# Memory cross-attention planned on all engines at once, and head 0 of its queries by plain products

## The chip, the cores and the metric

The kernel runs on one core of one Trainium2 chip. The metric is the device time of one execution in microseconds (us). Three runs of the kernel before gave 1443.65 to 1445.43 us, with a median of 1444.97 us.

The engines are named as in the profile: PE (TensorE, matmuls; PEld is its weight load), DVE (VectorE), ACT (ScalarE), POOL (GpSimd) and SP (SyncE, whose queue issues most of the DMAs; POOL issues those that add to what is in the tile already).

## What is computed

One sequence of 512 tokens with 1024 channels goes through two layers. Each has a mixer (attention of two kinds in layer 0, an mLSTM in layer 1), a cross-attention to a memory of 256 tokens, and a gated feed-forward part with a short convolution. The change is in the cross-attention, which has 4 heads of 256 channels:

```
def memory_cross_attention(xn, memn, wq, wkv, wo):
    q = split_heads(xn @ wq, XATTN_HEADS)
    k, v = jnp.split(memn @ wkv, 2, axis=-1)
    k = split_heads(k, XATTN_HEADS)
    v = split_heads(v, XATTN_HEADS)
    logits = jnp.einsum('bhqd,bhmd->bhqm', q, k, preferred_element_type=jnp.float32) * (XATTN_HEAD_DIM ** -0.5)
    p = jax.nn.softmax(logits, axis=-1)
    out = jnp.einsum('bhqm,bhmd->bhqd', p.astype(v.dtype), v)
    return merge_heads(out) @ wo
...
x = x + memory_cross_attention(rms_norm(x, xattn_norm[layer]), rms_norm(mem, mem_norm[layer]), ...)
```

## The kernel before

**Products.** Activations lie with channels on the 128 partitions: `x` is eight tiles `x0` to `x7` of 128x512. Every operand of a product is split into a high part of type fp32r and the rest, so that a product is three matmuls (`mm3`, lines 374 to 380: high by high, low activation by high weight, high activation by low weight). A block of 128 output channels needs a weight tile of 128x1024, which goes through three steps: a DMA into a `raw` tile, a cast on ACT into `wh`, a subtraction on DVE into `wl`. There are three buffers each of `raw`, `wh` and `wl`. PE writes to four banks `acc0` to `acc3`, and to two each of `s` and `w`.

**The stage.** In each layer the cross-attention begins where the mixer's output product ends. That product's last block gives `x7`: DVE adds it (`xadd`), ACT writes `xh7` and a square, DVE writes `xl7` and sums the squares (`xprep`). The stage has these parts:

- Values: two blocks of 512 channels, each from four weight tiles of `in_xv`, with `mem` as the other operand (`p_proj_tok`, lines 440 to 442, 512 columns a matmul), kept as `xvh` and `xvl`.
- Keys: eight blocks of 128 channels from `in_xk`. Four of them are computed within the mixer already (`p_fill`) and wait in two `acc` banks; DVE scales them (tile `u`), ACT and DVE split them into `kt`. The other four are computed within the stage.
- Queries: eight blocks of 128 channels from `in_xq`, two for each head. A pair of blocks is computed with seven products of half size instead of eight (`p_seven`, 256 columns a matmul). It needs sums of the pair's weight halves: the tile `sa`, loaded by SP and added to by a DMA of POOL, the tile `sb0` or `x0`, formed by DVE and added to by another DMA of POOL, and a plain half loaded into `x5`. It also needs sums of the activations' halves (`form`: tiles `q`, then `pth`, `ptl` and `mixed`). As the tiles of `x` serve as room for these weights, `x` is written to DRAM first (`xs`) and read back later.
- For each head and each 128 queries: scores (`s`), their maximum (`sm`), the exponential (`xe`), its division by the sum, a transposition (line 1393), the weighting of the values (`w`).
- Output: eight blocks from `in_xo`, added to `x`, whose parts the feed-forward part uses.

**What sets the order.** `Plan` (line 111) holds the stage's steps with a priority and a duration on PE, and a chain of what follows on ACT and DVE. It keeps a clock for PE, takes the ready step of the best priority, and calls its function, which issues the instructions of all engines at once. Priorities are written out: values `VP` = 5, the four pairs 10, 20, 30 and 40, weights of a pair `PREP` = 19 earlier, keys `KP` = 57, scores 55 to 85, output 100. The order that results is not fixed within an engine: the builder moves instructions of different steps against each other. The feed-forward part is ordered by another planner, `Sched` (line 208): each instruction or group is a task of its own engine with a duration, a due time, the tasks it needs and the buffers it takes and frees, and the order that it finds is fixed on ACT, DVE and POOL (`nc.planned(True)`).

Of the kernel before, what the change touches and what calls it, by code (L numbers as in the profile page):

```python
# [16 lines left out]
P = 128  # L17
SEQ = 512
# [66 lines left out]
KP = 57  # L85
PREP = 19
VP = 5
FORM_AT, FORM_STEP = 2.0, 5.0


class Busy:

    def __init__(self, free):
        self.free, self.spans = free, []

    def place(self, at, d):
        at = max(at, self.free)
        k = 0  # L100
        for k, (a, b) in enumerate(self.spans):
            if at + d <= a:
                break
            at = max(at, b)
        else:
            k = len(self.spans)
        self.spans.insert(k, (at, at + d))
        return at + d


class Plan:
# [3 lines left out]
    def __init__(self, prev=None, hold=(), gaps=False, **res):  # L115
        self.gaps = gaps
# [13 lines left out]
    def run(self):  # L130
        todo = sorted(self.items, key=lambda i: (i.prio, i.n))
        eng, t = self.eng, self.t
        busy = {e: Busy(min(eng[e], t + 0.5)) for e in eng}

        def place(e, at, d):
            if self.gaps:
                return busy[e].place(at, d)
            eng[e] = max(eng[e], at) + d
            return eng[e]

        while todo:
# [27 lines left out]
            for e, d in pick.pre:  # L169
                place(e, t - 4.0, d)  # L170
# [3 lines left out]
            for e, d in pick.chain:  # L174
                if e == "-":
                    u += d
                    continue
                u = place(e, u, d) + 0.06
                clear = clear or u
            for e, d in pick.load:  # L180
                place(e, t, d)
# [25 lines left out]

class Sched:
# [3 lines left out]
    def __init__(self, **res):  # L212
        self.tasks = []
# [9 lines left out]
    def slot(self, r):  # L223

        s = self.slots[r]
        if r == "acc":
            return min(range(len(s)), key=lambda i: s[i])
        return self.turn[r] % len(s)

    def run(self):  # L230
        order = sorted(self.tasks, key=lambda t: (t.prio, t.n))
# [7 lines left out]
        now = {e: -AHEAD.get(e, 0.0) for e in todo}  # L239
        inf = float("inf")  # L240
        idle = 0.0
        while any(todo.values()):
            best = None
            for e, ts in todo.items():
                soon, pick = inf, None
                for t in ts[:120]:
# [9 lines left out]
                    for r, _ in t.take:  # L256
# [3 lines left out]
                        at = max(at, self.slots[r][self.slot(r)])  # L260
# [66 lines left out]
class Builder:  # L327
# [830 lines left out]
    def form(self, layer, k, to, scratch):  # L1158

        nc, tt = self.nc, self.nc.vector.tensor_tensor  # L1160
        hi, lo, raw = (v[:].rearrange("p a b -> p (a b)") for v in to)
        for j in range(2):
            nc.scalar.activation(scratch[:, j, :], self.x[k + 4 * j][:], AF.Identity, scale=self.col("xat", layer * 8 + k + 4 * j))
        T1, T3, T2, T4 = (raw[:, 256 * i : 256 * i + 256] for i in range(4))
        x0, x1 = ([scratch[:, j, 256 * i : 256 * i + 256] for i in range(2)] for j in range(2))
        tt(out=T1, in0=x0[0], in1=x0[1], op=ALU.subtract)
        tt(out=T3, in0=x1[1], in1=x0[1], op=ALU.subtract)
        nc.vector.scalar_tensor_tensor(out=T2, in0=T1, scalar=-1.0, in1=x1[1], op0=ALU.mult, op1=ALU.subtract)
        nc.vector.scalar_tensor_tensor(out=T4, in0=T2, scalar=-1.0, in1=x1[0], op0=ALU.mult, op1=ALU.subtract)
        self.split(hi, lo, raw)  # L1170

    def p_seven(self, pl, pair, mp, X, T, formed, kdeps, done, prio, before, turn):
# [1022 lines left out]
```

## Time and profile before

| what | us |
|---|---|
| median of three runs | 1444.97 |
| profiled execution | 1446.33 |
| its span, first to last instruction | 1444.4 |
| PE busy within the span | 1411.4 |
| DVE, ACT, POOL busy | 1178.2, 865.8, 152.8 |
| cross-attention of layer 0 on PE | from 252.44 to 409.19 |
| cross-attention of layer 1 on PE | from 951.45 to 1107.23 |

The profile is that of one execution. A row of the timeline gives the start of an instruction, its duration, its engine and line, the tile written and those read, and in brackets the idle time before it with what ended it. Matmuls overlap, so that their durations add up to more than they take: a matmul's price is the distance between starts. A row of the windows gives the busy time of each engine in a stretch, and the clock that was granted to PE (1.00 is full). Times count from the span's start.

### The profile page before, as it was taken

The numbers are of one execution on the slowest core, as the hardware profiler recorded it, in microseconds if no ns is written. First come the engines' busy times: TensorE is split into PE (matmuls) and PEld (weight loads), VectorE is DVE, ScalarE is ACT, GpSimd is POOL, SyncE is SP. The second block draws the span as 40 slices with busy tenths as digits, with TensorE's granted clock in tenths as the row PEclk, the third lists the DMA queues.
The fourth block names the chain that finished last, engine by engine and source line by source line (L and its number), as shares of the span: only waits on it lengthen the run. The fifth ranks groups of instructions, "written<-read, shape, count | busy, mean of one in ns | idle before, by whom it ended". The sixth has DMA issues, their size and how long they took to land.

```text
span 1444.4 us, 23191 instructions
## 1 busy us (share of the span) xinstructions
PE 1411.4 (98%) x8732; PEld 1271.1 (88%) x8732; DVE 1178.2 (82%) x2018; ACT 865.8 (60%) x1456; POOL 152.8 (11%) x205
## 2 busy tenths in 40 slices
PE   9999999799999999999999999988999999999998
PEld 8888869699889999999888888877988899999997
DVE  7887776767789999999768867676767999999984
ACT  6797554555566665666456654464556666656654
POOL 0003220300001011110001121020000011110100
PEclk9999999899999999999999999999999999999999
DMA  5225325754148776774233332566504777676622
GB/s 203 87 67 162 95 86 188 214 139 146 60 143 216 187 186 173 190 181 120 74 113 110 117 110 66 168 198 173 174 5 136 206 198 191 176 187 170 158 74 80
DMA packets 78304, 206.85 MB, mean 143 GB/s; under 512 B 8449, under 2 KB 8449, under 8 KB 78193
## 3 DMA queue, kind: packets, MB, share of 16 engines
q1 hardware_dynamic: 62432, 163.97, 34.4%
q0 software_dynamic: 14752, 40.30, 16.0%
q8 instruction: 68, 1.11, 0.3%
q10 hardware_dynamic: 1008, 1.12, 0.2%
q14 instruction: 44, 0.35, 0.1%
HBM read 199.01 MB, written 6.34 MB: 142 GB/s over the span
## 4 chain that ended last, share of the span: by engine, by line
PE 83%; DVE 6%; ACT 3%; issue 3%; DMA 3%; POOL 1%; POOLq 0%; DVEq 0%; ACTq 0%; SPq 0%
PE acc L378 16%; PE acc L379 16%; PE acc L380 16%; PE w L379 5%; PE w L378 5%; PE w L380 5%; PE s L378 3%; PE s L380 3%; PE s L379 3%; PE acc L440 2%; PE acc L442 2%; PE acc L441 2%; DVE wl L300 1%; ACT wh L300 1%; PE w L1971 1%
## 5 line engine op out<-in xcount | busy, mean ns | idle before, releaser
L300 ACT CAST wh<-raw 128x1024 fp32r<-128x1024 f32 (+2 forms) x221 | 226.4, 1026 | 186.6 <-PE acc L379 94.7
L300 DVE TENSOR_TENSOR wl<-raw,wh 128x1024 fp32r<-128x1024 f32 (+2 forms) x221 | 264.4, 1198 | 40.9 <-ACT wh L300 40.5
L378 PE MATMUL acc<-xh,wh 128*128 128x512 f32 (+1 forms) x736 | 244.6, 332 | 0.0
L379 PE MATMUL acc<-xl,wh 128*128 128x512 f32 (+1 forms) x736 | 243.0, 330 | 0.0
L380 PE MATMUL acc<-xh,wl 128*128 128x512 f32 (+1 forms) x736 | 243.0, 330 | 0.0
L380 PEld LDWEIGHTS acc<-xh,wl 128*128 128x128 f32 x736 | 140.7, 191 | 10.2
L378 PEld LDWEIGHTS acc<-xh,wh 128*128 128x128 f32 x736 | 140.8, 191 | 10.0 <-DVE x L300 0.3
L379 PEld LDWEIGHTS acc<-xl,wh 128*128 128x128 f32 x736 | 140.8, 191 | 9.4
L300 DVE SCALAR_TENSOR_TENSOR c<-hs,vec,c 128x512 f32<-128x512 f32 x176 | 131.8, 749 | 3.8 <-ACT c L300 0.8
L378 PE MATMUL w<-ah,wh 128*128 128x512 f32 x304 | 115.7, 381 | 0.2 <-ACT c L300 0.2
L379 PE MATMUL w<-al,wh 128*128 128x512 f32 x304 | 115.2, 379 | 0.0
L380 PE MATMUL w<-ah,wl 128*128 128x512 f32 x304 | 115.2, 379 | 0.0
L300 ACT ACTIVATE c<-hs,vec 128x512 f32<-128x512 f32 x88 | 70.8, 812 | 12.2 <-DVE hs L300 8.0
L300 ACT CAST ah<-c 128x512 fp32r<-128x512 f32 x44 | 27.3, 620 | 84.0 <-DVE c L300 83.9
L300 DVE TENSOR_TENSOR x<-acc,x 128x512 f32<-128x512 f32 (+1 forms) x43 | 27.9, 653 | 52.9 <-PE acc L380 52.9
L378 PEld LDWEIGHTS w<-ah,wh 128*128 128x128 f32 x304 | 57.6, 190 | 7.9 <-DVE x L300 0.9
L380 PEld LDWEIGHTS w<-ah,wl 128*128 128x128 f32 x304 | 57.5, 189 | 8.1
L300 POOL TENSOR_TENSOR y<-z,power 128x4 f32<-128x4 f32 (+1 forms) x17 | 31.5, 1855 | 305.4 <-DVE z L300 305.3
L379 PEld LDWEIGHTS w<-al,wh 128*128 128x128 f32 x304 | 57.6, 190 | 6.5
L378 PE MATMUL acc<-mem,wh 128*128 128x256 f32 (+1 forms) x192 | 60.4, 315 | 2.8 <-ACT wh L300 2.7
L300 DVE TENSOR_TENSOR wl<-sa,wh 128x1024 fp32r<-128x1024 f32 x44 | 53.8, 1223 | 10.2 <-ACT wh L300 10.1
L300 POOL DMA_DIRECT2D sa<-in_up_dram x36 | 31.4, 873 | 279.6 <-DMA sa<-in_up_dram 121.9
(429 smaller groups left out, 4177.2 us busy)
## 6 DMA issues: line engine op xcount, KB each, us to landing
raw<-in_up_dram SPq DMA_DIRECT2D x52, 512.0 KB, 4.1
sa<-in_up_dram SPq DMA_DIRECT2D x36, 512.0 KB, 3.6
sa<-in_up_dram POOLq DMA_DIRECT2D x36, 512.0 KB, 6.5
raw<-in_down_dram SPq DMA_DIRECT2D x32, 512.0 KB, 4.0
ra<-in_up_dram SPq DMA_DIRECT2D x36, 256.0 KB, 4.3
sb<-in_up_dram POOLq DMA_DIRECT2D x36, 256.0 KB, 5.0
raw<-in_wo_dram SPq DMA_DIRECT2D x16, 512.0 KB, 4.2
raw<-in_xk_dram SPq DMA_DIRECT2D x16, 512.0 KB, 3.6
```

Of the source, the lines that this page charges most:

```text
L300: i = issue(*a, **k)
L378: mm(out, wh, xh, start=first, stop=False, skip_group_check=parts)
L379: mm(out, wh, xl, start=False, stop=False, skip_group_check=parts)
L380: mm(out, wl, xh, start=False, stop=last, skip_group_check=parts)
L440: mm(ps, xh[k][:, ts], wh, start=(k == 0), stop=False)
L441: mm(ps, xh[k][:, ts], wl, start=False, stop=False)
L442: mm(ps, xl[k][:, ts], wh, start=False, stop=(k == 7))
L1971: nc.tensor.matmul(ps[:, lo:], vv[s][:, c], a[:], start=(s == 0), stop=(s == 3))
```

## The change

The planner `Sched` gets three things. A task may take two buffers of one kind at once. Due times of ACT, DVE, POOL and SP tasks are no longer those written by hand but are computed (`dues`): a task's latest useful time is the earliest latest time of those that need it, or its buffer, less its duration; PE tasks keep theirs. And an engine may wait (`WAIT`, 0.4 us for DVE, 0.3 for ACT) for a task that is due earlier, instead of taking the first that can start.

The cross-attention is written anew as tasks of this planner (`xattn_steps`), with its own order of the PE work: 16 half-weight steps of the values (the first `ONE` = 4 come before the activations' sums in the list, the other `TWO` = 12 after), then head 0, then the pairs of heads 1, 2 and 3 by seven products with key blocks or the scores of head 0 between them, then transpositions and scores in turn with the weighting, then the output. Head 0 is now computed by plain products (`plain`): two weight tiles of `in_xq`, each with 24 matmuls of 512 columns, and no sums. The order is fixed on ACT, DVE and POOL for the whole stage. The mixers and the feed-forward parts stay as they were. `Plan` loses the search for gaps between planned spans.

In each layer PE has 36 instructions less in this stage, and DVE 8 less. The core of the diff:

```diff
+WAIT = {"DVE": 0.4, "ACT": 0.3}
+ONE, TWO, FORM, THEN = 4, 12, 10.0, (2, 1, 1)
...
+    def dues(self):
+        after = {t.n: [(c, 0.0) for c in ()] for t in self.tasks}
+        for t in self.tasks:
+            for d in t.deps:
+                after[d.n].append((t, 0.0 if d.eng == t.eng else d.lat))
...
+        def last(t):
+            if t.n not in late:
+                late[t.n] = t.prio
+                ends = [last(c) - lat for c, lat in after[t.n]]
+                if ends and t.eng != "PE":
+                    late[t.n] = min(ends) - t.dur
+            return late[t.n]
...
-                    if at < soon - 1e-6:
-                        soon, pick = at, t
-                if pick is not None and (best is None or soon < best[0]):
-                    best = (soon, e, pick)
+                    able.append((at, t))
+                if able:
+                    near = min(at for at, _ in able) + self.wait.get(e, 0.0) + 1e-6
+                    soon, pick = next((at, t) for at, t in able if at <= near)
...
+        sc = Sched(
+            WAIT, raw=3, h=3, sa=2, sb=2, ra=1, s2=1, a22=1, s4=1, qc=1, v=1, u2=1, u3=1, kx=1, q=6, kt=3, e=7, pt=2, acc=4, s=2, w=2
         )
+        sc.slots.update(h=[-10.4, -5.2, 0.0])
...
+            return add("SP", 0.0017 * cols, fn, (), at, [(tag, st)], (), 4.0)
...
+        sc.ahead = {**AHEAD, "ACT": 10.4, "DVE": 10.4}
+        for at in (-10.4, -5.2, 0.0):
+            add("DVE", 0.65, None, (), -40.0, after=at + 0.2)
+            add("ACT", 1.2, None, (), -40.0, after=at + 1.0)
+            add("DVE", 1.3, None, (), -40.0, after=at + 1.8)
+        XLAST = 3.0
...
+        def keys(m, get, deps, free=()):
...
+                st["x"] = self.til(mp, "kx", (P, MEM), bufs=1)
+                tt_(out=folded(st["x"][:]), in0=restored(get()), in1=folded(self.memrb[:]), op=ALU.mult)
...
+        def plain(p):
+            sts, qs, los = [], ({}, {}), []
+            for j in range(2):
+                st, lo = weight(t["xq"][layer, 2 * p + j], clock[0])
+                last = None
+                for c in range(4):
...
+                        for k in (2 * c, 2 * c + 1):
+                            w = slice(k * P, (k + 1) * P)
+                            self.mm3(st["ps"][:], st["wh"][:, w], st["wl"][:, w], self.xh[k], self.xl[k], k == 0, k == 7)
+                    last = pe(1.297, fn, [lo, last], [("acc", st)] if c == 0 else (), [("h", st)] if c == 3 else ())
...
+        some(ONE)
+        for k in range(4):
+            f, a, st = form(k, FORM + 4.0 * k)
...
+        some(TWO)
+        for _ in plain(0):
+            pass
+        got.append(seven(1, lambda i: some(THEN[i])))
+        got.append(seven(2, lambda i: scores(0, i)))
+        scores(0, 3)
+        got.append(seven(3, lambda i: some((2, 1, 1)[i])))
...
+        for m in range(8):
+            for _ in out_block(m):
+                pass
+        nc.planned(True)
+        sc.run()
+        nc.planned(False)
```

In the new kernel the DVE multiplication that scales a key block writes a tile `kx` with one buffer, where the kernel before had four buffers `u`.

**How the order moves.** Outside the two stages the order of the engines stays the same, but for a few instructions where the stage meets the feed-forward part. The number behind a name tells which of many tiles of that name it is; line 300 in the kernel before and line 306 in the new one are the helper that records each operation of DVE, ACT and POOL.

On DVE, where the stage begins in layer 0, the kernel before has the following rows. `wl_2808` is the low part of the first value weight, `x_144` is `x7` with the addition of the mixer's output, the four `u` are the key blocks that wait in `acc`, and `z` is a small step of the normalization.

```order
L300 SCALAR_TENSOR_TENSOR xl_555_2696<-x_142,vec,xh_554_2695 128x512
L300 TENSOR_TENSOR x_143<-acc_553_2688,x_143 128x512
L300 TENSOR_TENSOR wl_2808<-raw_2806,wh_2807 128x1024
L300 SCALAR_TENSOR_TENSOR xl_562_2736<-x_143,vec,xh_561_2735 128x512
L300 TENSOR_TENSOR sq_2551<-sq_2551,sqt_2739 128x512
L300 TENSOR_TENSOR x_144<-acc_560_2728,x_144 128x512
L300 TENSOR_TENSOR u_2786<-acc_512_2421,memrb_1933 128x256
...
L300 SCALAR_TENSOR_TENSOR xl_565_2763<-x_144,vec,xh_564_2762 128x512
L300 TENSOR_TENSOR sq_2551<-sq_2551,sqt_2766 128x512
L300 TENSOR_TENSOR kt_2785<-u_2786,kt_2785 128x256
...
L300 TENSOR_TENSOR wl_2853<-raw_2851,wh_2852 128x1024
```

In the new kernel the same place reads as follows; the first value weight is `wl_2809`, and `kx` is the tile that takes the place of `u`.

```order
L306 SCALAR_TENSOR_TENSOR xl_562_2736<-x_143,vec,xh_561_2735 128x512
L306 TENSOR_TENSOR sq_2551<-sq_2551,sqt_2739 128x512
L306 TENSOR_TENSOR x_144<-acc_560_2728,x_144 128x512
L306 TENSOR_TENSOR kx_2804<-acc_512_2421,memrb_1933 128x256
L306 TENSOR_TENSOR wl_2809<-raw_2797,wh_2808 128x1024
L306 SCALAR_TENSOR_TENSOR xl_565_2763<-x_144,vec,xh_564_2762 128x512
L306 TENSOR_TENSOR sq_2551<-sq_2551,sqt_2766 128x512
L306 TENSOR_TENSOR kt_2803<-kx_2804,kt_2803 128x256
L306 TENSOR_TENSOR kx_2816<-acc_512_2421,memrb_1933 128x256
L306 TENSOR_TENSOR wl_2821<-raw_2799,wh_2820 128x1024
```

The first value weight's subtraction moved from a place ahead of the addition of `x7` to one behind it and behind the first key block's multiplication. The second value weight's moved from a place behind all four key blocks' splitting to one behind the first block's.

On SP's queue at the same place the kernel before has these rows; `sa` are the loads of the pairs' sums, `xs` is the copy of `x7` to DRAM, and `x_625` is a plain half.

```order
L363 DMA raw_2869<-in_xv_dram 128x1024
L1209 DMA sa_2776<-in_xq_dram 128x2x512
L1209 DMA sa_2803<-in_xq_dram 128x2x512
L1289 DMA xs_633_3005<-x_144 128x512
L1230 DMA x_625_2985<-in_xq_dram 128x512
L363 DMA raw_2903<-in_xv_dram 128x1024
L363 DMA raw_2932<-in_xv_dram 128x1024
L363 DMA raw_3007<-in_xv_dram 128x1024
L363 DMA raw_3025<-in_xv_dram 128x1024
L363 DMA raw_3043<-in_xv_dram 128x1024
```

In the new kernel the same place of SP's queue has these.

```order
L1193 DMA sa_2806<-in_xq_dram 128x2x512
L1193 DMA sa_2812<-in_xq_dram 128x2x512
L1193 DMA raw_2818<-in_xv_dram 128x1024
L1304 DMA xs_665_3096<-x_144 128x512
L1193 DMA raw_2826<-in_xv_dram 128x1024
L1193 DMA raw_2855<-in_xv_dram 128x1024
L1193 DMA raw_2884<-in_xv_dram 128x1024
L1193 DMA x_644_3003<-in_xq_dram 128x512
L1193 DMA raw_2913<-in_xv_dram 128x1024
L1193 DMA raw_2954<-in_xq_dram 128x1024
```

Three value weights moved ahead of the plain half, and behind the last of them the weight of head 0 (`raw_2954` from `in_xq`) follows at once.

On POOL the kernel before has these rows in the stage of layer 0: the sums that its DMAs add (`sa`, `sb`) and the small root of the normalization (`y`).

```order
L300 DMA sa_2776<-in_xq_dram 128x1024
L300 DMA sa_2803<-in_xq_dram 128x1024
L300 TENSOR_TENSOR y_2832<-z_2831,power 128x4
L300 DMA sb_608_2915<-in_xq_dram 128x512
L300 DMA sa_3090<-in_xq_dram 128x1024
```

In the new kernel they are these.

```order
L306 DMA sa_2806<-in_xq_dram 128x1024
L306 DMA sa_2812<-in_xq_dram 128x1024
L306 DMA x_658_3069<-in_xq_dram 128x512
L306 TENSOR_TENSOR y_3144<-z_3143,power 128x4
L306 DMA sa_3140<-in_xq_dram 128x1024
```

The first addition to a half (`x_658`) moved ahead of the root, and the root stands behind three DMAs in place of two.

More of the change, by code (lines that the diff above doesn't have):

```diff
@@ L84, with __init__ @@
 HOLD = 4.0
[L85 to L108, printed above, removed]
 class Plan:
-    def __init__(self, prev=None, hold=(), gaps=False, **res):
-        self.gaps = gaps
+    def __init__(self, prev=None, hold=(), **res):
         self.items = []
@@ L238, in run @@
                 want[r].append(t)
-        now = {e: -AHEAD.get(e, 0.0) for e in todo}
+        now = {e: -self.ahead.get(e, 0.0) for e in todo}
         inf = float("inf")
```

658 lines of the change are left out of this document (420 added, 238 removed).

## The prediction

> **What bounds the kernel now.** First the page's head, for the execution's length and each engine's load.
>
> ```profile
> span 1444.4 us, 23191 instructions
> PE 1411.4 (98%) x8732; PEld 1271.1 (88%) x8732; DVE 1178.2 (82%) x2018; ACT 865.8 (60%) x1456; POOL 152.8 (11%) x205
> ```
>
> PE is busy for 98% of the span, so the change can only gain in two ways: less work for PE, or PE's work done without gaps and without lost clock. The whole span's share doesn't tell where the cross-attention stands, so I went next to PE's timeline, for the first matmul of the stage (line 440) and the first of the feed-forward part (line 378 with `xh`), in both layers.
>
> ```profile
> 252.44 0.38 PE L440 MATMUL acc<-wh,mem 128*128 128x512 f32 x1
> ...
> 409.19 0.38 PE L378 MATMUL acc<-xh,wh 128*128 128x512 f32 x1
> ...
> 951.45 0.38 PE L440 MATMUL acc<-wh,mem 128*128 128x512 f32 x1
> ...
> 1107.23 0.38 PE L378 MATMUL acc<-xh,wh 128*128 128x512 f32 x1
> ```
>
> The stage takes 409.19 − 252.44 = 156.75 us in layer 0 and 155.78 in layer 1. What it would take without any loss needs the price of a step. Four rows of the same timeline, each pair inside a run of matmuls of one size, give it as a distance of starts.
>
> ```profile
> 239.71 0.38 PE L379 MATMUL acc<-ml,wh 128*128 128x512 f32 x1
> 251.79 0.38 PE L378 MATMUL acc<-qa,wh 128*128 128x512 f32 x1
> ...
> 321.89 0.28 PE L379 MATMUL acc<-ptl,x 128*128 128x256 f32 x1
> 323.90 0.28 PE L379 MATMUL acc<-mixed,x 128*128 128x256 f32 x1
> ```
>
> Fifty-six steps of 512 columns lie between the first two (12.08 / 56 = 0.2157 us), eighteen of 256 columns between the others (2.01 / 18 = 0.1117 us). By the code the stage has 336 steps of 512 columns (values 96, output 192, weighting 48): 72.5 us. It has 528 of 256 columns (four pairs of 84, keys 96, scores 96): 59.0 us. Transpositions and small sums add an estimated 4.4, from the size of their outputs. Together 135.9, so 20.9 us are lost in layer 0 and 19.9 in layer 1. Where they are lost the windows tell (columns: stretch, length, busy PE, PEld, DVE, ACT, POOL, PE's clock, DMA share, GB/s).
>
> ```profile
> core 0: us, PE busy (x) PEld busy (x) DVE busy (x) ACT busy (x) POOL busy (x), PEclk, DMA share, GB/s
> 252.40:292.00 39.60, 32.05 (x140) 26.89 (x140) 29.61 (x50) 23.38 (x33) 11.26 (x5) 0.83 0.72 201
> 292.00:344.00 52.00, 50.21 (x431) 48.85 (x430) 37.31 (x65) 30.52 (x56) 3.42 (x4) 1.00 0.60 175
> 344.00:409.20 65.20, 64.16 (x339) 55.63 (x338) 44.64 (x99) 32.39 (x69) 0.14 (x2) 1.00 0.23 74
> 409.20:442.00 32.80, 32.80 (x157) 28.86 (x156) 31.79 (x52) 23.93 (x32) 2.96 (x3) 1.00 0.54 161
> 259.70:264.70 5.00, 5.00 (x12) 3.96 (x13) 4.83 (x9) 2.68 (x4) 5.00 (x1) 0.50 1.04 268
> 279.20:285.20 6.00, 6.00 (x26) 5.82 (x27) 4.39 (x6) 3.13 (x4) 0.84 (x1) 0.50 0.69 156
> ...
> 951.40:992.00 40.60, 32.74 (x148) 26.79 (x148) 31.15 (x51) 24.32 (x35) 11.42 (x5) 0.87 0.75 216
> ```
>
> The first 40 us hold the loss: PE idle for 39.60 − 32.05 = 7.55 us (7.86 in layer 1), and at half clock for 5.0 + 6.0 us, which costs another 5.5. The other two windows are idle for 1.79 and 1.04 us; the remaining 20.9 − 7.55 − 5.5 − 2.83 ≈ 5.0 must lie in gaps that the modelled ends of matmuls cover. The fourth window is the feed-forward part, ordered by the planner that now gets this stage: no idle time at all. What ends the waits is in PE's waits of the first window and in its timeline, with layer 1's longest.
>
> ```profile
> PE acc L440 <- ACT wh L300: 4.1, 1, 4.1
> PE acc L441 <- DVE wl L300: 3.1, 2, 2.5
> ...
> 256.15 1.05 PE L537 MATMUL s<-ones,sq 128*128 128x2 f32 x8 [0.33 <-DVE sq L300]
> 259.70 0.79 PE L441 MATMUL acc<-wl,mem 128*128 128x512 f32 x1 [2.50 <-DVE wl L300]
> 279.16 1.22 PE L440 MATMUL acc<-wh,mem 128*128 128x512 f32 x2 [4.14 <-ACT wh L300]
> 304.33 0.38 PE L378 MATMUL acc<-mem,wh 128*128 128x256 f32 x1 [1.66 <-ACT wh L300]
> ...
> 987.79 0.48 PE L441 MATMUL acc<-wl,mem 128*128 128x512 f32 x1 [3.28 <-DVE wl L300]
> ```
>
> PE waits for value weights: their splitting on DVE is late, or their raw tile is. So the stage's beginning is bound by the preparation of weights, the rest by PE.
>
> **The change, part by part.** *Plain head 0.* Seven products are 84 × 0.1117 = 9.38 us, the plain pair 48 × 0.2157 = 10.35: PE gets 0.97 us a layer more, and the new floor is 136.8 us. The sums of head 0, one POOL DMA of 512 KB and one of 256 KB are gone; DVE and ACT, 29.61 and 23.38 of 39.60 us busy there, get lighter just where they are late. I cost that at nothing beside the 0.97.
>
> *Start of the stage.* These rows of DVE and ACT give the durations.
>
> ```profile
> 248.34 1.23 DVE L300 TENSOR_TENSOR wl<-raw,wh 128x1024 fp32r<-128x1024 f32 x1 [0.18 <-ACT wh L300]
> 252.64 0.69 DVE L300 TENSOR_TENSOR x<-acc,x 128x512 f32<-128x512 f32 x1 [1.82 <-PE acc L380]
> 253.25 1.41 DVE L300 TENSOR_TENSOR u<-acc,memrb 128x256 f32<-128x256 f32 x4
> ...
> 252.43 1.05 ACT L300 CAST wh<-raw 128x1024 fp32r<-128x1024 f32 x1 [2.99 <-PE acc L379]
> ```
>
> Before, the first value weight's subtraction ran at 248.34, while the mixer's product still occupied PE. Now it stands behind the addition of `x7`, which cannot start before 252.64, and behind one key block's multiplication. It ends at 252.64 + 0.61 (distance to the next start) + 0.35 (a quarter of 1.41) + 1.23 = 254.8. PE wants it after two steps, at 252.9: a wait of about 2.0 us, which is new and comes once a layer. Queued behind it on DVE are `xl7` and the sum of squares, which the normalization needs; nobody on PE needs those before the first pair or plain head, some 40 us on.
>
> *The other value weights.* Before, the next one was subtracted only behind all four key blocks and part of the sums (row at 259.70: a wait of 2.50). Now only the first block stands ahead of it, so this wait goes, and the half clock behind it. Next late is the ring of three raw tiles. Each weight feeds 12 × 0.2157 = 2.59 us of matmuls, so a round of three is 7.8 us. A raw tile's round is its landing, a cast of 1.05, a subtraction of 1.23 and about 0.2 between: the landing plus 2.5. The landings, by DMA issues of the raw tiles from 225 to 330 us, were these (all raw tiles, then value weights alone).
>
> ```profile
> DMA to landing us min/median/max: 3.1/3.8/6.2
> ...
> raw<-in_xv_dram SPq DMA_DIRECT2D x8, 512.0 KB, 4.9
> ```
>
> With 4.9 the ring's round is 7.4 us, below 7.8, and holds; with 6.2 it is 8.7. DVE's own work from the addition of `x7` to the last value weight is eight subtractions at 1.23 and about 10 us of splitting and sums in some 21 us; it nearly fills the time. I book one further slip of 1.2 us, an estimate from that tightness: 2.0 + 1.2 = 3.2 us lost here, between 2 (the ring never late) and 10 (late each round).
>
> *Middle and end.* Before, 1.79 + 1.04 us of idle time and 5.0 hidden were lost. DVE is busy for 37.31 of 52.00 and 44.64 of 65.20 us there; a planned order should find PE's work in time, as in the fourth window, but the end (weighting, then output) runs through DVE and ACT a head at a time, and its short gaps are of the kind that stay. I keep the 2.8 and a third of the 5.0: 4.5, with 2 and 8 as ends.
>
> *POOL.* Its additions to the tiles of the pairs now stand around the root `y` in another order (first `x`, then `y`, then the third `sa`). The rows that price it, and the same root in the feed-forward part:
>
> ```profile
> 257.59 7.83 POOL L300 TENSOR_TENSOR y<-z,power 128x4 f32<-128x4 f32 x1
> ...
> 415.97 1.21 POOL L300 TENSOR_TENSOR y<-z,power 128x4 f32<-128x4 f32 x1 [36.62 <-DVE z L300]
> ```
>
> A DMA queued behind it waits for up to 7.83 us. The first pair's products come only after 41 us of values and 10 us of plain products, so I take nothing; the other end is the last rival.
>
> *Sum.* Lost after: 3.2 + 4.5 = 7.7 us a layer. Layer 0 gains 20.9 − 7.7 − 0.97 = 12.2, layer 1, which loses the same way, 19.9 − 7.7 − 0.97 = 11.2; together 23.4. The profiled execution, 1446.33 us (span 1444.4 and 1.9 around it), would be 1422.9. It lies 1.36 above the median of the runs, so the median becomes **1421.6 us**. By the ends of the terms, 4 to 18 us lost a layer, it is 1414 to 1442; both at their far end together is unlikely, and the forecast's own range is 1414 to 1430.
>
> **Rivals.** *The new first wait halves the clock.* For it: the wait of 2.50 us did (0.50 until 264.70), and 2.0 is not far off. Against: the wait of 1.66 at 304.33 lies in a window whose clock is 1.00. Just ahead of the 2.50 stood a microsecond of tiny sums (row at 256.15), which the new wait doesn't have. Price as there, 5.0 us at half clock, so 2.5 a layer: 1426.6. [...]
>
> *Transfers in each other's way.* SP now issues value weights, `sa`, the plain half and the weights of head 0 closely, where the DMA share was 1.04 already in one stretch. With landings of 6.2 the ring loses 0.9 us on each of its remaining two rounds, and the waits may reach 4 with one stretch at half clock (3.0 us): about 9.4 us lost at the start in place of 3.2, so 6.2 a layer more: 1434.
>
> *All is better placed than I think.* Start 2, rest 2: 3.7 us a layer less, 1414, and somewhat lower if the ring's wait vanishes with it.
>
> *The freed time is not PE's to use.* The end runs through DVE and ACT, which gain little; if gaps there take what the start frees, the kernel stays at 1445. Against: 44.64 of 65.20 us on DVE.
>
> *Slower: the sums of the pairs come late.* Place: POOL's queue, where the third `sa` stands behind `y`, and the `x` that SP loads wait for the copy of `x7`. If the root is asked for late, or its 7.83 us repeat at each turn, the pairs' products wait. It decides from the point where a sum lands over 2.5 us after PE has reached its product, for then the clock halves too. Three pairs at the 4.14 us of the longest wait with its 3.0 us of half clock are 21 us; with 4 us at the start and 4.5 at the end a layer loses 29.5 + 0.97, against 20.9 and 19.9: about 10 us a layer slower, 1465.
>
> **How the numbers follow.** Forecast 0.52; better than it 0.12; half clock 0.12; transfers 0.10; no use 0.06; slower 0.08. The median of three runs here spreads by 1.8 us, so 0.2% (2.9 us) is about what a measurement can tell from no change. Faster by more than that takes the first four, 0.86, less some for their upper ends that reach 1442 and beyond: 0.83. Within it 0.06; slower 0.11, the last rival and 0.03 of those ends. The range takes the forecast, most of the better case, half clock and transfers: 1411 to 1438.
>
> **What would show it.** Right: the stages at about 144.5 us each; a wait of about 2 us for the first `wl` right at the stage's start and none over 2.5 behind it; clock 1.00 from the second value weight on; PE idle below 5 us in the first 40; the matmuls of head 0 0.2157 us apart. Wrong: a stage above 150 us; waits of line 380's products for `sa` or `x` that POOL adds to; DVE over 90% busy at the end with PE waiting for it; any change outside the two stages by more than 2 us.

## The result, and the profile after

The changed kernel took 1424.22 us (median of four runs, 1422.05 to 1424.72) against 1444.31 (four runs of the kernel before); the ratio is 0.9858, with a 95% interval of 0.984 to 0.9875. That is 20.1 us less. The prediction was 1421.6 us, 23.4 less than the median it started from.

The page of the changed kernel begins so.

```profile
span 1422.3 us, 22959 instructions
...
PE 1399.5 (98%) x8660; PEld 1263.0 (89%) x8660; DVE 1169.5 (82%) x2006; ACT 859.9 (60%) x1444; POOL 138.4 (10%) x201
```

PE's timeline gives the stage as before; line 1375 is now the first matmul of the values, and the second and fifth row are the first of head 0's plain products.

```profile
254.45 0.38 PE L1375 MATMUL acc<-wh,mem 128*128 128x512 f32 x1
...
281.96 0.38 PE L384 MATMUL acc<-xh,wh 128*128 128x512 f32 x1
...
398.35 0.38 PE L384 MATMUL acc<-xh,wh 128*128 128x512 f32 x1
...
940.61 0.38 PE L1375 MATMUL acc<-wh,mem 128*128 128x512 f32 x1
...
968.12 0.38 PE L384 MATMUL acc<-xh,wh 128*128 128x512 f32 x1
...
1084.51 0.38 PE L384 MATMUL acc<-xh,wh 128*128 128x512 f32 x1
```

The stage takes 143.90 us in both layers, where it took 156.75 and 155.78: 12.85 and 11.88 less, 24.7 together. Between the stages the two kernels take the same 542.26 us. The spans differ by 22.1, since in this execution the first stage begins 2.01 us later than in that of before (254.45 against 252.44) and the part behind the second takes 0.6 more. The experiments below begin the first stage between 252.03 and 253.12, but for e12, whose stage begins with a gap. The 2.01 us arise well ahead of the stage, 0.8 of them before 13 us, where both kernels run the same code; why, no run shows. So medians that differ by some 2 us need not differ in the stage, and below the length of the stage stands beside the median where it matters.

The windows of the stage in layer 0, and the start of the one in layer 1, show where.

```profile
core 0: us, PE busy (x) PEld busy (x) DVE busy (x) ACT busy (x) POOL busy (x), PEclk, DMA share, GB/s
254.40:294.90 40.50, 36.21 (x177) 30.38 (x177) 35.66 (x55) 28.07 (x39) 4.38 (x4) 1.00 0.74 217
294.90:344.00 49.10, 49.06 (x429) 48.53 (x428) 36.94 (x84) 30.73 (x65) 3.37 (x4) 1.00 0.56 165
344.00:398.30 54.30, 54.05 (x268) 47.29 (x267) 36.78 (x72) 25.68 (x48) 0.17 (x2) 1.00 0.24 78
...
940.60:981.00 40.40, 36.38 (x176) 30.22 (x175) 35.69 (x55) 28.18 (x39) 4.38 (x4) 1.00 0.74 210
```

PE's clock is 1.00 in all of them, where the first window had 0.83. PE's idle time in the first window falls from 7.55 to 4.29 us, in the second from 1.79 to 0.04, in the third from 1.04 to 0.25. In the first window DVE is now busy for 88% of the time in place of 75%: the same engine has less empty time in the part where PE waits for it.

What is left at the start stands in PE's waits of the first window (us in total, times, longest).

```profile
PE acc L1376 <- DVE wl L306: 2.7, 4, 1.0
PE acc L1375 <- ACT wh L306: 1.0, 1, 1.0
PE acc L1375 <- DVE x L306: 0.6, 1, 0.6
```

The first two of them in PE's timeline:

```profile
255.40 0.48 PE L1375 MATMUL acc<-wh,mem 128*128 128x512 f32 x1 [0.57 <-DVE x L306]
256.86 0.48 PE L1376 MATMUL acc<-wl,mem 128*128 128x512 f32 x1 [0.98 <-DVE wl L306]
```

And DVE's timeline at the same place:

```profile
254.65 0.69 DVE L306 TENSOR_TENSOR x<-acc,x 128x512 f32<-128x512 f32 x1 [2.34 <-PE acc L386]
255.26 0.41 DVE L306 TENSOR_TENSOR kx<-acc,memrb 128x256 f32<-128x256 f32 x1
255.59 1.22 DVE L306 TENSOR_TENSOR wl<-raw,wh 128x1024 fp32r<-128x1024 f32 x1
256.72 0.75 DVE L306 SCALAR_TENSOR_TENSOR xl<-x,vec,xh 128x512 fp32r<-128x512 f32 x1
```

The first subtraction runs where the prediction put it: behind the addition of `x7` and one key block. PE does two steps of 0.2157 between 254.45 and 256.86, so it loses 1.98 us there; 2.0 was forecast. A part of it was not seen: the second matmul of the stage, for the other 128 tokens of the memory, needs a bank that the addition of `x7` still reads (the wait of 0.57).

### The profile page after: what moved, and what is told of

Same layout as the page of the kernel before. It is cut to its first block, busy times and chain, and to the rows that moved or that the text cites. A ratio compares the mean times of both kernels' runs of the same rounds, so it can differ in the third digit from the quotient of the medians.

```text
span 1422.3 us, 22959 instructions
## 1 busy us (share of the span) xinstructions
PE 1399.5 (98%) x8660; PEld 1263.0 (89%) x8660; DVE 1169.5 (82%) x2006; ACT 859.9 (60%) x1444; POOL 138.4 (10%) x201
## 4 chain that ended last, share of the span: by engine, by line
PE 83%; DVE 9%; ACT 3%; issue 2%; DMA 2%; POOL 0%; POOLq 0%; DVEq 0%; ACTq 0%
PE acc L384 17%; PE acc L385 17%; PE acc L386 17%; PE w L384 4%; PE w L386 4%; PE w L385 4%; PE s L384 3%; PE s L386 3%; PE s L385 3%; DVE wl L306 2%; PE acc L446 1%; PE acc L448 1%; PE acc L447 1%; DMA raw<-in_xv_dram 1%; PE w L2244 1%
## 5 line engine op out<-in xcount | busy, mean ns | idle before, releaser
L384 PE MATMUL acc<-xh,wh 128*128 128x512 f32 (+1 forms) x752 | 251.7, 335 | 0.0
L386 PE MATMUL acc<-xh,wl 128*128 128x512 f32 (+1 forms) x752 | 250.1, 333 | 0.0
L385 PE MATMUL acc<-xl,wh 128*128 128x512 f32 (+1 forms) x752 | 250.1, 333 | 0.0
L386 PEld LDWEIGHTS acc<-xh,wl 128*128 128x128 f32 x752 | 143.1, 190 | 11.1
L385 PE MATMUL w<-al,wh 128*128 128x512 f32 x304 | 115.2, 379 | 0.0
L386 PE MATMUL w<-ah,wl 128*128 128x512 f32 x304 | 115.2, 379 | 0.0
L386 PE MATMUL acc<-mem,wl 128*128 128x256 f32 (+1 forms) x192 | 59.6, 310 | 1.1 <-DVE wl L306 1.1
L384 PE MATMUL acc<-mem,wh 128*128 128x256 f32 (+1 forms) x192 | 59.6, 310 | 0.1
L385 PE MATMUL acc<-mem,wh 128*128 128x256 f32 (+1 forms) x192 | 59.5, 310 | 0.0
```

The costliest lines, as they stand in the source:

```text
L384: mm(out, wh, xh, start=first, stop=False, skip_group_check=parts)
L385: mm(out, wh, xl, start=False, stop=False, skip_group_check=parts)
L386: mm(out, wl, xh, start=False, stop=last, skip_group_check=parts)
```

## The experiments

Times are medians, with the range of the runs in brackets; the expectation is the one written ahead of the run. The kernel before was timed beside them, at 1443.7 us (e1 to e4), 1444.25 (e5 to e8) and 1444.98 (e9 to e12).

**e1: head 0 by seven products again, in the new order.**

```diff
-        for _ in plain(0):
-            pass
-        got.append(seven(1, lambda i: some(THEN[i])))
+        got.append(seven(0, lambda i: some((1, 1, 1)[i])))
+        got.append(seven(1, lambda i: some((1, 1, 1)[i])))
```

> The new order with head 0 by seven products again (the key blocks spread over all four pairs as fillers). Theory 1, the gain is the order's and plain products only trade PE work for lighter DVE and ACT: PE has 0.97 us a layer less, but the four pairs have fewer fillers and the first sums are wanted 10 us earlier, an estimate of 1 to 4 us more waiting a layer; 1422 to 1431 us. Theory 2, the plain products carry the gain because the first sums cannot be ready after 27.5 us of values: waits of 4 us with half clock behind them as before, so 6 us or more a layer; 1436 us or more.

1424.7 us (1421.45 to 1426.98), ratio to the kernel before 0.9866 (0.985 to 0.9882), the same as with plain products. Its stages take 145.44 and 144.35 us, 2.0 more together than those of the changed kernel, and most of that can be one stretch at half clock (3.41 us at 0.50; its rows stand under e8). Theory 1 holds: in the new order the plain products are worth nothing that the medians can tell.

**e2, e5 and e9: plain head 0 alone, in the order of before.**

```diff
+                if h == 0:
+                    for j in range(2):
...
+                        qe = [self.p_proj(pl, t["xq"][layer, j], lambda: (self.xh, self.xl), plain, ...)]
+                    continue
                 e, steps = self.p_seven(
```

> The kernel before with nothing changed but head 0, by two plain blocks. Theory 1, the order carries the gain: DVE still does all four key blocks ahead of the second value weight, so the wait of 2.50 us and its half clock stay; plain products add 0.97 us a layer and take away at most the 4.14 us wait: 1438 to 1447 us. Theory 2, the lighter DVE, ACT and POOL carry it: 1434 us or less.

> The kernel before with head 0 by two plain blocks, as in the run before it, but with pair 1's weights laid over the tiles of x only when the sums of x are formed (in that run they were laid there too early, which left head 1 without its right operands). Theory 1, the order carries the gain and the plain products none: 1440 to 1447 us. Theory 2, the plain products help the old order too, and that run hid it: 1434 us or less.

> The kernel before with head 0 by two plain blocks, now with each pair's first sum of weights kept back until the pair ahead has used its own (in the two runs before, a pair's weights were written over those of the pair ahead, an argument from the code; this run shows whether that was all). Theory 1, the order carries the gain: 1440 to 1447 us. Theory 2, the plain products carry it: 1434 us or less.

e5 and e9 also hold back one step of each pair, until the sums of the activations are formed (e5) and besides until the pair ahead has used its own (e9).

1444.51, 1442.0 and 1443.47 us; the ratios are 1.0005 (0.9996 to 1.0015), 0.9991 (0.998 to 1.0002) and 0.9994 (0.9982 to 1.0006). The times fall where theory 1 has them. But none of the three computes what the kernel before computes, so some step of theirs must take its data too early or too late. Which one is not known. The reasons given in the expectations of e5 and e9 were not the whole of it, since the kernel is no better with them mended; nor is it seen at `qc`, the pair's sum, for in the trace of e9 each pair's four writes to `qc` stand ahead of its two copies. No instruction is left out, but some waits may be missing and others may be new, so these times are a hint and no proof. PE's waits in the stage of layer 0 of e9 are these.

```profile
PE acc L441 <- DVE wl L300: 3.1, 2, 2.5
PE s L378 <- DVE qc L300: 2.6, 2, 2.4
PE acc L440 <- ACT wh L300: 2.2, 1, 2.2
```

The wait of 2.5 us for the second value weight stands as it did, 4.1 us for another has become 2.2, and 2.6 us of waiting behind a pair's sum `qc` have come in (3.5 in layer 1, each with a stretch at half clock behind it). If that fault made those, a sound version could be faster by as much, some 9.5 us (2.6, 3.5 and 1.7 for each stretch, an estimate from the 3.41 us at 0.50 of e1 and e3), which reaches the 1434 us of theory 2. So e1 is the run that tells the plain products from the order, and it does so for the new order only.

**e10: one place of DVE's order alone.** In the kernel before, the four key blocks were held back on the planner's clock.

```diff
                                 lambda keys=keys, st=st, m=m: keys(st["ps"], at=m % 2 * MEM), 0, (), 0, ...
+                                after=pl.t + 2.0 * (m + 1),
```

> The kernel before, with the four key blocks that wait in acc held back 2 us each by the planner's clock, so that the second value weight's subtraction stands on DVE behind the first block only, as in the changed kernel. Theory 1, this place alone makes the first loss (a wait of 2.50 us and 2.5 us of half clock in each layer): about 8 us less, 1436 us. Theory 2, the wait only moves to the next value weights, which stand behind the sums: 1443 us or more.

1448.82 us, ratio 1.0028 (1.0016 to 1.0041): slower by 0.3%. This kernel, too, does not compute what the kernel before does, and why is not known. PE's timeline in layer 0:

```profile
260.56 0.48 PE L441 MATMUL acc<-wl,mem 128*128 128x512 f32 x1 [0.68 <-DVE wl L300]
...
269.98 1.22 PE L440 MATMUL acc<-wh,mem 128*128 128x512 f32 x2 [6.56 <-ACT wh L300]
```

The wait of 2.50 us is gone, as meant, and a wait of 6.56 us for a later value weight, with half clock behind it (the two matmuls of its row take 1.22 us, as those of the kernel before at 279.16, where the clock is 0.50), has come in its place. That is theory 2, that one place mended moves the wait on to the next weights, with the reservation that this kernel takes some data too early or too late.

**e11 and e12: the planner's two new rules, each taken away.**

```diff
-        if self.wait:
-            self.dues()
```

```diff
-WAIT = {"DVE": 0.4, "ACT": 0.3}
+WAIT = {"DVE": 0.0, "ACT": 0.0}
```

> The changed kernel with the due times written by hand, without the computed latest useful times; the wait of 0.4 and 0.3 us stays. On DVE the third value weight's subtraction then stands behind all four key blocks, 1.2 us later. Theory 1, the tasks' order of the new stage carries most of the gain: 1424 to 1428 us. Theory 2, the computed times carry it: 1434 us or more.

> The changed kernel with computed due times but without the readiness to wait 0.4 and 0.3 us. On DVE the first value weight's subtraction then stands behind seven instructions from x7's addition on in place of two, about 2.5 us later. Theory 1, that makes the first wait 4.5 us, enough for the half clock (2.5 us more): 4 to 5 us a layer, 1432 to 1434 us. Theory 2, the ring's slow landing hides it, since the next weights land meanwhile: 1425 to 1428 us.

e11 (the first edit): 1426.9 us, ratio 0.9886 (0.987 to 0.9901). e12: 1422.84 us, ratio 0.9858 (0.9841 to 0.9875). The computed due times carry some 3 us of the gain by the medians (4.4 by the stages, which take 146.26 and 145.91 us in e11); the readiness to wait carries nothing that the medians can tell. Both taken away together were not run. In e12 the first wait grew, but at another place than forecast: PE's small sums of squares (`sq`) now stand ahead of the first value step and wait for DVE. With it came the half clock that the first rival of the prediction named:

```profile
255.39 1.05 PE L1256 MATMUL s<-ones,sq 128*128 128x2 f32 x8 [2.93 <-DVE sq L306]
```

The window behind it has PE's clock at 0.50:

```profile
257.90:260.90 3.00, 3.00 (x8) 2.32 (x7) 2.47 (x5) 1.29 (x3) 0.00 (x0) 0.50 0.99 242
```

In layer 0 it cost nothing in the end. PE had waited for the third and later value weights anyway, and now reached them when they had landed; behind 262 us there is no wait left up to the end of the stage. From the end of the mixer's last matmul to the feed-forward part are 143.0 us, where the changed kernel has 143.90. In layer 1 the same wait has 6.83 us of half clock behind it (940.43 to 947.26), and this stretch takes 146.07 us, 2.2 more. So the loss at the start and the loss in the ring overlap and are not two terms to be added, but a longer loss at the start is not free either.

**e4: the sums' loads later.** The loads of `sa` follow the value weights on SP's queue.

```diff
             b1 = load(sa, "sa", w.rearrange("j r c -> r j c")[:, :, :512], 1024, at - 20.0, sa_tile, True)
+            b1.after = 8.0
...
+                if tag == "sa":
+                    nc.sync.follow()
                 nc.sync.dma_start(to.rearrange("p (a b) -> p a b", a=2) if pairs else to, src)
```

> The changed kernel, but the loads of the pairs' sums stand behind the fourth further value weight and behind the plain weights on SP's queue, not ahead of all of them. Theory 1, these 2 MB of loads and additions hold up the value weights, which take 5.9 us to land: the landing falls to about 4.5 us and the waits for the later value weights (2.3 us of idle time and about 1.5 hidden a layer) mostly go: 1417 to 1421 us. Theory 2, DVE's work sets the pace of the value part: no change, 1424 us. Theory 3, the sums now come too late for pair 1: a wait of 2 to 5 us behind the plain products, 1426 to 1432 us.

1416.4 us (1415.78 to 1420.64), ratio 0.9817 (0.9801 to 0.9833): a little below what theory 1 gave, and clear of the changed kernel's interval. The DMA issues from 252 to 282 us (KB each, median us to landing) of the changed kernel

```profile
raw<-in_xv_dram SPq DMA_DIRECT2D x5, 512.0 KB, 5.9
...
sa<-in_xq_dram SPq DMA_DIRECT2D x2, 512.0 KB, 4.3
sa<-in_xq_dram POOLq DMA_DIRECT2D x2, 512.0 KB, 8.5
```

and of e4

```profile
raw<-in_xv_dram SPq DMA_DIRECT2D x5, 512.0 KB, 3.6
...
sa<-in_xq_dram SPq DMA_DIRECT2D x2, 512.0 KB, 6.1
sa<-in_xq_dram POOLq DMA_DIRECT2D x2, 512.0 KB, 7.9
```

differ by 2.3 us in the landing of a value weight. The waits of e4 up to the plain products are 1.3 us for `wl` and 0.6 for the bank: of the ring's waits 0.3 us are left, the first wait has stayed. The stage takes 141.1 us in each layer, 2.8 less than in the changed kernel. The edit moves the loads of SP and the additions of POOL that follow them, so it does not tell which of the two held up the value weights.

**e3: the high parts first.** Each value weight's eight steps that need only `wh` run ahead of the four that need `wl`.

```diff
                         for i in range(2):
...
                             mm(ps, xh[k][:, ts], wh, start=(k == 0), stop=False)
-                            mm(ps, xh[k][:, ts], wl, start=False, stop=False)
                             mm(ps, xl[k][:, ts], wh, start=False, stop=(k == 7))
+                            late.append((ps, xh[k][:, ts], wl, k == 7))
+                        if k2:
+                            for ps, x, wl, stop in late:
+                                mm(ps, x, wl, start=False, stop=stop)
```

> The changed kernel, but of each value weight's twelve steps the eight that need only the high part go first and the four with the low part last; nothing else moves. Theory 1, the subtraction on DVE ends late and PE loses the time: waits for wl of 2.7 us and the first wait of 2.0 shrink by about 3 us a layer: 1418 us. Theory 2, the raw tiles' landing is the end of the value part: only the tail behind the last weight gets shorter, 1.7 us a layer: 1420.8 us. Theory 3, the wait for wl only turns into a wait for wh: 1424 us.

1420.99 us (1420.4 to 1421.62). That theory 2 gave 1420.8 is luck: its stages take 143.75 and 143.17 us, only 0.9 less together than those of the changed kernel, and the rest of the difference lies in front of and behind them. PE's waits up to 300 us:

```profile
PE acc L1377 <- ACT wh L306: 2.6, 2, 2.0
PE acc L1382 <- DVE wl L306: 0.3, 1, 0.3
```

The waits for `wl` fell from 2.7 to 0.3 us, those for `wh` rose from 1.0 to 2.6: most of it was the landing, and the wait changed its name, which is theory 3's mechanism. The wait of 2.0 us in layer 0 also brought a stretch at half clock (its rows stand under e8). The intervals of the ratios overlap (0.9826 to 0.9859 here), the runs themselves don't.

**e6 and e7: both, and the key blocks later.** e6 is e3 and e4 together; e7 is e6 with this besides:

```diff
-            a = add("DVE", tt(256), scaled, deps, clock[0] + 0.5, take, free)
+            a = add("DVE", tt(256), scaled, deps, clock[0] + 0.5, take, free, after=2.0 if m < 4 else -99.0)
```

> The changed kernel with the later loads of the sums and with the eight steps of each value weight that need only the high part ahead of the four with the low part. Theory 1, the first wait (2.0 us) and the slow landing are losses of their own: the later loads alone gave 1416.4, and of the 2.0 about 1.3 and of later waits 0.4 us a layer go: 1413 us. Theory 2, the new order of the steps only gained where weights landed late, and that is gone now: 1416 us.

> As the run before it, and the four key blocks that wait in acc are scaled no earlier than 2 us into the stage by the planner's clock, so that the first value weight's subtraction stands ahead of the addition of x7 as in the kernel before. Theory 1, the first wait is DVE's order alone: the rest of it, about 0.6 us a layer, goes too: 1412 us. Theory 2, the key blocks then hold their two acc banks longer and the second value block waits for them, 1 to 2 us a layer: 1414 us or more.

e6: 1421.28 us (1417.21 to 1428.08), ratio 0.9853 (0.9826 to 0.988), above either theory: a new wait, for a weight of head 0, as its timeline shows in layer 1.

```profile
963.79 0.48 PE L385 MATMUL acc<-xh,wh 128*128 128x512 f32 x1 [2.30 <-ACT wh L306]
```

The window behind it:

```profile
964.40:967.40 3.00, 3.00 (x9) 2.34 (x8) 3.00 (x6) 3.00 (x5) 0.87 (x1) 0.50 0.81 231
```

The values end earlier there, and by SP's order the weights of head 0 now stand among the loads of the sums; behind these 2.30 us the clock halves. Whether it does differs from execution to execution: the fastest of the five runs had a mean clock of 1.000, the slowest 0.994. e7: 1410.23 us (1409.98 to 1410.48), ratio 0.977 (0.9751 to 0.9789), 14 us below the changed kernel and the best version of these. Its stage takes 138.37 and 138.38 us, 1.6 above the floor of 136.8 and 11.1 together below the changed kernel's. The window of its first 40 us:

```profile
252.20:292.20 40.00, 40.00 (x222) 35.58 (x221) 37.50 (x58) 29.60 (x42) 3.47 (x4) 1.00 0.77 225
```

DVE's timeline around the start of the stage:

```profile
242.97 1.23 DVE L306 TENSOR_TENSOR wl<-raw,wh 128x1024 fp32r<-128x1024 f32 x1 [0.21 <-ACT wh L306]
...
248.11 1.23 DVE L306 TENSOR_TENSOR wl<-raw,wh 128x1024 fp32r<-128x1024 f32 x1 [0.18 <-ACT wh L306]
...
252.42 0.69 DVE L306 TENSOR_TENSOR x<-acc,x 128x512 f32<-128x512 f32 x1 [1.82 <-PE acc L387]
253.28 1.23 DVE L306 TENSOR_TENSOR wl<-raw,wh 128x1024 fp32r<-128x1024 f32 x1 [0.17 <-ACT wh L306]
```

PE is not idle at all in the first 40 us. The edit did more than its expectation says. Counted along the ring from their loads, the first value weight is subtracted at 242.97 and the second at 248.11, both inside the mixer's product, where the kernel before has only the first; the third follows right behind the addition of `x7`. Each frees a raw tile, so the load of the fourth value weight goes out at 244.22, and at 256.87 in the changed kernel. The wait that theory 2 feared did not come, and the gain is larger than theory 1 has it: what went with the first wait was the late start of the ring, which theory 1 did not name. How much each of the two is worth was not run.

**e8: the clock and a gap without small matmuls.** The last value weight's subtraction is repeated, three more times in layer 0 (the last on 640 columns), four more in layer 1.

```diff
+                if nh == 1 and c == 3:
+                    def again(once=lo.fn, s=st):
+                        for cols in ((1024, 1024, 640), (1024, 1024, 1024, 1024))[layer]:
+                            self.sub(s["wl"][:, :cols], s["raw"][:, :cols], s["wh"][:, :cols])
+                        once()
+                    lo.fn = again
```

> The changed kernel with the last value weight's subtraction repeated, so that PE meets one idle gap without any small matmuls in it: about 2.8 us in layer 0 (three more, the last of 640 columns), about 4.3 us in layer 1 (four more). [...] Theory 2, 2.50 us are enough: half clock behind both. Time in either case 1424 plus about 2.2 and 3.6 us for the gaps and 2.5 for each stretch at half clock: 1432.5 or 1435 us, less what the next weights' earlier readiness gives back.

1431.96 us. In layer 0 it missed its aim: other work filled the gap, 0.73 us of it was left. In layer 1 the gap was 3.56 us and the clock halved behind it. The two times of the expectation differ by a stretch at half clock behind a gap of some 2.8 us in layer 0, which no run shows. Other waits came unplanned, at the fifth value weight of layer 0 of several kernels. In e8 the clock halved there behind two short waits (0.50 from 269.80 to 272.40):

```profile
266.27 0.38 PE L1385 MATMUL acc<-wh,mem 128*128 128x512 f32 x1
268.01 0.48 PE L1383 MATMUL acc<-wh,mem 128*128 128x512 f32 x1 [1.36 <-ACT wh L306]
269.27 0.80 PE L1384 MATMUL acc<-wl,mem 128*128 128x512 f32 x1 [0.78 <-DVE wl L306]
```

In e1 it halved (0.50 from 269.80 to 273.21) behind almost the same two waits as in the changed kernel, which kept its clock (1.00). First e1, then the changed kernel:

```profile
268.33 0.48 PE L1375 MATMUL acc<-wh,mem 128*128 128x512 f32 x1 [1.15 <-ACT wh L306]
269.60 0.63 PE L1376 MATMUL acc<-wl,mem 128*128 128x512 f32 x1 [0.78 <-DVE wl L306]
```

```profile
269.55 0.48 PE L1375 MATMUL acc<-wh,mem 128*128 128x512 f32 x1 [1.04 <-ACT wh L306]
270.81 0.48 PE L1376 MATMUL acc<-wl,mem 128*128 128x512 f32 x1 [0.78 <-DVE wl L306]
```

In e3 the clock halved behind a wait of 2.0 us (the longest in its waits above). So the length of the longest wait alone does not tell these kernels apart: 1.66 us left the clock at 1.00 in the kernel before, 1.15 us in e1 did not. In the trace of the kernel before, the nine instants at which the granted clock changes, from 258.00 to 1442.42 us, lie whole multiples of 3.41 us apart (347 times 3.413 us from the first to the last). Cut where the clock changes, the windows of e1 and of e3 are:

```profile
266.39:269.80 3.41, 1.48 (x6) 0.76 (x5) 1.49 (x3) 2.56 (x5) 0.00 (x0) 1.00 0.94 380
269.80:273.21 3.41, 3.41 (x9) 2.69 (x9) 3.41 (x7) 3.41 (x6) 0.00 (x0) 0.50 0.58 163
```

```profile
265.39:268.80 3.41, 1.42 (x7) 0.94 (x6) 0.88 (x1) 1.96 (x3) 0.00 (x0) 1.00 0.99 389
268.80:272.21 3.41, 3.41 (x10) 2.69 (x9) 3.41 (x8) 3.41 (x6) 0.00 (x0) 0.50 0.60 184
```

and those of the changed kernel, whose clock changes only at its very end (1420.38), cut by the same step counted back from there, are:

```profile
266.68:270.09 3.41, 2.32 (x10) 1.45 (x8) 0.68 (x2) 1.64 (x3) 0.00 (x0) 1.00 1.02 408
270.09:273.50 3.41, 2.69 (x12) 2.38 (x13) 3.41 (x8) 3.41 (x6) 0.00 (x0) 1.00 0.67 222
```

In e1 both waits fall into one window, which leaves PE busy for 1.48 of 3.41 us, and the next window is at 0.50. In the changed kernel the cut at 270.09 lies between the two waits, neither window has PE busy for less than 2.32 us, and the clock stays at 1.00. That this made the difference between the two is the author's estimate from these rows; no run was made to show it.

## Why the prediction was right, point by point

- **The floor and the stage.** 136.8 us of work and 7.7 lost were forecast, 144.5 us a layer; the stage took 143.90, so 7.1 are lost. That the sum came so near is in part luck, for the two terms of the loss were off in opposite directions: 3.2 at the start was 5.9 (27.51 us from the first value step to the first plain one, less 96 x 0.2157 and 0.95 of sums), and 4.5 for the rest was 1.2 (116.39 us, less 115.2 of work). By its stages alone the kernel gained 24.7 us, 1.3 more than the 23.4 forecast. The profiled execution, 1424.06 us, lies above the 1422.9 forecast for it all the same, because of the 2.01 and 0.6 us outside the stages. The prediction named a change of more than 2 us there as a sign against it; this one is just over that and is not explained.
- **The first wait**, 2.0 us: 1.98, at the place named. That it simply adds to the loss was not right: e12 made the loss there longer, and layer 0 lost nothing more, layer 1 2.2 us.
- **The ring**, forecast to hold with a landing of 4.9 us and one slip of 1.2: it landed in 5.9 and lost 3.9. The rival of transfers in each other's way, priced at 6.2 us a layer, was half true: e4 shows the sums' loads as its cause, at 2.8 us of stage time a layer. The landing of 4.9 is where this term went wrong. It is the median of eight weights, three of which are loaded ahead of the stage. By the same measure (225 to 330 us) the changed kernel has 4.7, so the figure did not get worse, it was the wrong one; the five weights loaded within the stage (252 to 282 us) took 5.4 us in the kernel before already, with which the ring's round is 7.9 us, above the 7.8 that it must keep. The rows are, for the changed kernel from 225 to 330 us and for the kernel before from 252 to 282:

```profile
raw<-in_xv_dram SPq DMA_DIRECT2D x8, 512.0 KB, 4.7
...
raw<-in_xv_dram SPq DMA_DIRECT2D x5, 512.0 KB, 5.4
```

- **The rest**, 4.5: the idle time of 2.83 us fell to 0.29, and most of the 5.0 hidden went with it. The weighting and the output keep PE busy when their order is planned, with DVE busy for 75 and 68% of these windows.
- **Plain head 0**, 0.97 us and no gain: e1 finds no difference in the medians.
- **POOL's root**, taken at nothing: it ran for 2.54 us and nothing on PE waited for it. The working of this point had a slip: the values are 96 steps, 20.7 us, and not 41 us, so the sums of pair 1 were needed some 20 us earlier than it says, and were there.
- **The half clock of the first rival** stayed away in the changed kernel's trace (1.00 in the windows of the stage). With almost the same waits at the fifth value weight (1.15 and 0.78 us, where the changed kernel has 1.04 and 0.78) it came in e1, and it came in e3, e6, e8 and e12. Here the prediction's "clock 1.00" held without a reason that it gave, and why it held is only estimated, under e8.
- **The planner.** The fourth window of the prediction, the feed-forward part without idle time, was the right guide to what the stage would become. Taking away its new rules one at a time changes little (e11, e12), and mending one place of the old order changed nothing for the better (e10, with the reservation made there). That leaves the stage's new order of PE's steps, with the order of ACT, DVE and POOL fixed to it; these two were not separated.

## What to carry to other kernels

A wait at one weight of a ring, mended by itself, reappeared here at a later one (2.50 us went and 6.56 came in e10); price the ring as a whole, from the loads within the stretch in question, and don't add a wait at its head to the waits within it. Look at what shares the DMAs with the transfers that the next 20 us need: loads that are wanted 30 us later cost 2.8 us a layer here by standing ahead of them (a value weight landed in 5.9 us with them ahead, in 3.6 without). When the low part of a split weight is late, the steps that need only the high part can go first, but here, where the landing was last, that gained only 0.9 us of stage time in both layers together (e3: waits for the low part from 2.7 to 0.3 us, for the high part from 1.0 to 2.6).

## What the runs showed of the hardware

PE's granted clock fell to 0.50 at waits of PE of 4.14, 3.28 and 2.50 us in the kernel before, 2.93 us in e12, 2.30 us in e6 and 2.0 us in e3, and at pairs of short waits: 1.36 and 0.78 us in e8, 1.15 and 0.78 us in e1. It stayed at 1.00 at a wait of 1.66 us in the kernel before and at 1.04 and 0.78 us in the changed one. Within the stages of the kernel before it was 0.50 three times for 6.83 us and once for 3.41 (258.00 to 264.82, 278.48 to 285.30, 957.73 to 964.55 and 988.45 to 991.86), in e1 and e3 for 3.41 us each in the rows above. It differs between executions of one kernel: the five of e6 had mean clocks from 0.994 to 1.000. One stretch of 3.41 us full of matmuls costs about 1.7 us, an estimate from the granted 0.50.

POOL's small root, 7.83 us in the kernel before, took this in the changed one:

```profile
293.14 2.54 POOL L306 TENSOR_TENSOR y<-z,power 128x4 f32<-128x4 f32 x1 [3.85 <-DVE z L306]
```

What makes it that uneven, no run here tells apart.
